# A repeating load for the first norm's weights, scale-and-add steps for three residual rows, and five smaller reorderings in a two-layer hybrid trunk

## The chip, the core and the metric

The kernel runs on one core of one Trainium2 chip. A core has five engines that run their own instruction queues: TensorE (PE, matrix products into PSUM), VectorE (DVE), ScalarE (ACT), GpSimd (POOL) and SyncE (SP, which here issues the transfers). The metric is the device time of one execution in microseconds (us), lower is better; several runs of the kernel are given and the median counts. A profile comes from one execution of its own.

## The reference

Input x is 1024 tokens by 1024 channels in float32. Two layers follow, each `x <- x + RMSNorm_post(mixer(RMSNorm_pre(x)))`:

```python
def rms_norm(x, g):
    y = xf * lax.rsqrt(jnp.mean(xf * xf, axis=-1, keepdims=True) + EPS) * g

def dilated_attention_mixer(h, w_in, w_out, rel_bias):     # layer 0
    proj = h @ w_in                                        # q, k, v for 3 dilations, and a gate z
    ...                                                    # three dilated sliding windows, 16 heads of 64
    o = jnp.sum(wts[..., None] * jnp.stack(outs), axis=0)  # mixed by softmax over the log-sum-exps
    return (o * jax.nn.silu(z)) @ w_out

def s5_mixer(h, w_in, a_re, ..., w_glu, b_glu, w_out):     # layer 1
    u, z = proj[..., :SSM_WIDTH], proj[..., SSM_WIDTH:]
    y = s5_scan(u, ...)                                    # 64 groups of 16 channels, 64 complex states each
    g = jax.nn.gelu(y)
    y = g * jax.nn.sigmoid(g @ w_glu + b_glu)
    return (y * jax.nn.silu(z)) @ w_out
```

## The kernel before

Tokens are worked in eight rows of 128 (row 0 to row 7). Float32 precision is kept by splitting every operand into a high part (an ACT cast to fp32r, L109, L194, L287: `hh`, `whi`) and a low part (a subtraction, L110, L195, L288: `hl`, `wlo`), and by three matmuls per product: high by high, low by high, high by low. The program is one Tile program: a scheduler places the instructions on each engine's queue from data flow, priorities and a simulated timeline, so an edit in one place moves neighbours in others. `issue_after(i)` adds one edge: what is issued inside comes behind instruction `i` on the engine of `i`.

The stages that the change touches, in order of time:

- **The start** (0 to 30 us). Eight transfers of x rows, four quarters of the first value weights `w_v` (`raw_first`), the identity matrix `ident` and the first norm's weights are issued by SP. The norm's weights (1024 numbers) come as two rows of 512 on one partition (`grow`, L1007) and are spread over the 128 partitions by a matmul with a column of ones (`pg`, L1029) and two ACT copies (L182). Six matmuls on zeros (`idle`, L1014) stand on PE before these and six behind. `first_row` (L176) normalises row 0: ACT square with a running sum (L173), the reciprocal root on DVE in nine small steps (`rstd`, L94 to L101), the scaling by root and weights (L189), transposes on PE against `identr` (L152), ACT high part (L194), DVE low part (L195). `first_values` (L273) multiplies each row with the value weights (`psv`, L310), and lets the next rows' norms (`norm_transpose0`) run ahead.
- **Gates and values** (up to 330 us). `gates` projects the branch gate; its weights for four column blocks are loaded and split behind an instruction remembered as `c.behind`. `Quads.values` multiplies the rest of the values with seven products in place of eight, and interleaves jobs of `Prep`, which makes the state-space layer's tables: powers of the transition on DVE and POOL. `Prep.powers(et)` (L1709 ff.) needs block `et` of the input `bc`, loaded at L1650 into one of four work tiles `o[0..3]` or into a spare tile `c.vextra`; o[0] first holds a table that must have been stored to HBM (`tab_dr`, L1639).
- **Attention output** (`out_tiles`, L1232, about 1090 to 1210 us): per row two halves of the output product, then `out_norm` (L1196): ACT squares, `rstd`, DVE `y = ps*r*post` (L1208), POOL `x = x + y` (L1212).
- **The state-space layer** (`layer1`): 32 projection steps, with the stages of eight groups (`ssm_states`, `ssm_outputs`) appended to numbered steps by the list `at`. Group 7 is cut in halves; its second half `ssm_states1` runs at step `LAST_HALF` = 27. A half is: `pv` on PE, three products `T` on DVE, a sum on POOL (L1833), four scans on DVE (L1836), a product on POOL (L1838) and on DVE (L1841), and `X` (L1842), which the output product `py` (L1856) reads. The outputs go through a GELU: ACT (L1857, L1858), POOL (L1859, L1860), ACT tanh (L1861), DVE (L1862).
- **The last output product** (`out_units`, L1363): units of four output rows by seven products; `OutUnit.sums` (L1345) adds the products up in PSUM banks (`ow`, `ox`, `oy`, `oz`) with DVE L1343. All rows but the last use `out_norm` (in the last unit with half of the scaling on ACT L1210 and POOL L1211, `dve=False`), the last one `out_norm_last` (L1215).

Of the kernel before, what the change touches and what calls it, by code (L numbers as in the profile page):

```python
# [24 lines left out]
P = 128  # L25
# [3 lines left out]
H = 512  # L29
# [6 lines left out]

IDLE = 6

# [136 lines left out]

def first_row(c, x, x1, sq, grow, pgs, h, splits):  # L176

    nc = c.nc
    act, dve = Behind(c), Behind(c)
    act(lambda: square(c, 0, x, sq))  # L180
    for b in range(2):
        act(lambda: nc.scalar.copy(grow[:, b * H:b * H + H], pgs[b]))  # L182
    act(splits[0][0])
# [96 lines left out]
def first_values(c, a, rows):  # L280
# [13 lines left out]
    for i in range(8):  # L294
# [17 lines left out]
        with c.tc.issue_after(done[min(i + 2, 7)]):  # L312
            nc.scalar.copy(ev, ps)
        nc.sync.dma_start(c.v_dr[0, 0, i * P:i * P + P], ev)


# [665 lines left out]
def attention(c, a):  # L982
# [4 lines left out]
    with tc.tile_pool(name="vphase", bufs=1, side="right", reuse_waits="tile") as pool:  # L987
# [16 lines left out]

        grow, ones = [c.slot("grow", tag="b")[0:1] for _ in range(2)], c.slot("ones", tag="a")[0:1, 0:P]
        for n, t in enumerate(grow):
            nc.sync.dma_start(t, bass.AP(src.tensor, src.offset + n * H, [[0, 1], [1, H]]))  # L1007

# [7 lines left out]
        wait(IDLE)  # L1016
        nc.vector.memset(ones, 1.0)
        ident = c.slot("ident")[:, 0:P]
        nc.sync.dma_start(ident, a["ident"])
        c.raw_first = [x[:, 2 * n:2 * n + 2] for x in (c.vslot(4, F32), c.vslot(5, F32)) for n in range(2)]  # L1020
        for n in range(4):
            if n == 2:
                load_x(1)
            nc.sync.dma_start(c.raw_first[n], a["w_v"][0, n])
        load_x(2)
        nc.vector.tensor_copy(c.identr, ident)
        pgs = [c.pst.tile([P, H], F32, tag="pst", name="pg") for _ in range(2)]
        for ps, t in zip(pgs, grow):
            last = nc.tensor.matmul(ps, ones, t, start=True, stop=True)  # L1029
        with tc.issue_after(last.ins):  # L1030
            wait(IDLE)

        def rows(i, splits=None):
            if 2 < i + 2 < 8:
                load_x(i + 2)
            if i == 0:
                return first_row(c, xs[0], xs[1], sq, gain, pgs, h[0], splits)
            norm_transpose0(c, i, xs[i], sq, gain, h[i // 4], slice(i % 4 * P, i % 4 * P + P))
# [156 lines left out]

def out_norm(c, pss, post, x, eps=EPS, slot=None, dve=True, bank=None):  # L1196

# [3 lines left out]
    for n in range(2):  # L1201
        nc.scalar.activation(ys[n], pss[n], AF.Square, accum_out=ss[:, n:n + 1])
    r = rstd(c, ss, eps, bank)
    for n in range(2):
        ns = slice(n * H, n * H + H)
        y = ys[n]
        if dve or n == 0:
            nc.vector.scalar_tensor_tensor(y, pss[n], r[:, 0:1], post[:, ns], op0=ALU.mult, op1=ALU.mult)  # L1208
        else:
            nc.scalar.activation(y, pss[n], AF.Copy, scale=r[:, 0:1])  # L1210
            nc.gpsimd.tensor_tensor(y, y, post[:, ns], op=ALU.mult)  # L1211
# [20 lines left out]
def out_tiles(c, g, w, post, res, done, order, late):  # L1232
# [7 lines left out]
    for i in range(8):  # L1240
# [8 lines left out]
        c.nc.sync.dma_start(x, res(i))  # L1249
        out_norm(c, pss[i], post, x)  # L1250
        done(i, x)
# [49 lines left out]
class OutUnit:  # L1301
# [43 lines left out]
    def sums(self, i, slot):  # L1345
# [8 lines left out]
        elif i == 2:  # L1354
            self.add(self.Z, self.p0, self.Z)
        self.done.add(i)
# [4 lines left out]
def out_units(c, y, forms, post, res, done, last, eps, slot):  # L1361
# [13 lines left out]
    for n, (u, i) in enumerate(todo):  # L1375
# [8 lines left out]
        if i in ((3 if u.r == 3 else 4), 2):  # L1384
# [3 lines left out]
            if n + 1 == len(todo):  # L1388
                return out_norm_last(c, pss, post, x, lambda ns: last(x, ns), eps, slot, small)
            out_norm(c, pss, post, x, eps, slot, u.r < 3, small)  # L1390
            done(row, x)
# [201 lines left out]
class Prep:  # L1593
# [4 lines left out]
    def __init__(self, c, a, v):  # L1598
# [44 lines left out]
        self.mask, self.dd = o[2][:, 832:848], o[2][:, 848:864]  # L1643
        nc.vector.tensor_copy(self.mask, c.ident[:, 0:16])
        for n in range(1, 8):
            nc.vector.tensor_tensor(self.mask, self.mask, c.ident[:, 16 * n:16 * n + 16], op=ALU.add)
        self.tmp = o[3][:, 0:576]
        self.raw = {}
        for et, n, t in ((0, 4, o[0]), (4, 1, o[2][:, 576:832]), (5, 1, c.vextra), (6, 2, o[1][:, 0:512])):
            nc.sync.dma_start(t.rearrange("p (e x) -> p e x", e=n), a["bc"][:, et:et + n])  # L1650
# [224 lines left out]
def layer1(c, a, h1, ws):  # L1875
# [20 lines left out]
    for e in range(8):  # L1896
        t = (11 * e + 2) // 4
        for stage, d in ((ssm_loads, (-1, 2)[e] if e < 2 else 3), (ssm_input, 4 + (e == 0)), (ssm_taps, 6),
                         (ssm_states, 6 + (e == 0)), (ssm_outputs, 10)):
            at[t + d + 1].append((stage, e))  # L1900
    at[LAST_HALF + 1].append((ssm_states1, 7))

# [240 lines left out]
```

## Time and profile before

| | before |
|---|---|
| runs | 1593.5, 1597.0, 1595.37 us |
| median | 1595.37 us |
| the profiled execution | 1593.75 us, of which the span 1592.0 us |
| TensorE clock granted in it | 0.998 of full |
| PE busy | 1571.9 us (99%) |
| DVE, ACT, POOL busy | 1092.4, 826.1, 722.7 us |

A row of the timeline reads: start, duration, engine, line, operation, output tile <- input tiles, shape and count, and in brackets the idle time of the engine before it with what ended it. Matmuls overlap in the pipeline, so a matmul's duration is longer than the distance to the next one's start: rows of one kind are paced by their starts. "SPq" rows are the issue of a transfer, not the transfer.

### The profile page before, as it was taken

The numbers are of one execution on the slowest core, as the hardware profiler recorded it, in microseconds if no ns is written. First come the engines' busy times: TensorE is split into PE (matmuls) and PEld (weight loads), VectorE is DVE, ScalarE is ACT, GpSimd is POOL, SyncE is SP. The second block draws the span as 40 slices with busy tenths as digits, with TensorE's granted clock in tenths as the row PEclk, the third lists the DMA queues.
The fourth block names the chain that finished last, engine by engine and source line by source line (L and its number), as shares of the span: only waits on it lengthen the run. The fifth ranks groups of instructions, "written<-read, shape, count | busy, mean of one in ns | idle before, by whom it ended". The sixth has DMA issues, their size and how long they took to land.

```text
span 1592.0 us, 26875 instructions
## 1 busy us (share of the span) xinstructions
PE 1571.9 (99%) x9390; PEld 1327.6 (83%) x9390; DVE 1092.4 (69%) x2588; ACT 826.1 (52%) x2039; POOL 722.7 (45%) x603
## 2 busy tenths in 40 slices
PE   9999999999999999999999999999999999999997
PEld 6889999988888888888888888888888888878876
DVE  8799898945555655655655656659562999858576
ACT  5231223337777677767777677755453233335343
POOL 0000001026568677686777778711220455423466
PEclk9999999999999999999999999999999999999999
DMA  6313444433223333414324333448246888677513
GB/s 260 126 48 113 159 154 134 150 124 91 70 71 106 103 91 105 110 61 115 100 72 122 100 104 106 134 140 246 98 159 187 250 249 248 197 232 243 153 50 136
DMA packets 185808, 219.58 MB, mean 138 GB/s; under 512 B 43059, under 2 KB 139078, under 8 KB 185160
## 3 DMA queue, kind: packets, MB, share of 16 engines
q1 hardware_dynamic: 185672, 217.86, 44.7%
q8 instruction: 74, 1.21, 0.3%
q14 instruction: 62, 0.51, 0.1%
HBM read 158.75 MB, written 59.06 MB: 137 GB/s over the span
## 4 chain that ended last, share of the span: by engine, by line
PE 81%; DVE 8%; DMA 4%; POOL 3%; issue 2%; SPq 1%; ACT 1%; DVEq 0%; POOLq 0%; ACTq 0%
PE x L574 16%; PE psj L135 15%; PE y L574 12%; PE psq L453 10%; PE pso L1181 6%; PE pso L746 5%; PE psl L669 5%; PE pt L697 4%; PE psv L310 2%; PE psb L135 1%; DVE T L1836 1%; PE oz L1338 1%; PE ox L1338 1%; DVE T L1841 1%; PE pst L152 1%
## 5 line engine op out<-in xcount | busy, mean ns | idle before, releaser
L110 POOL TENSOR_TENSOR wqk<-wraw,wqk 128x512 fp32r<-128x512 f32 x161 | 214.0, 1337 | 101.4 <-ACT wqk L109 99.1
L691 ACT ACTIVATE lg<-lg,nm 128x128 f32<-128x128 f32 (+1 forms) x384 | 168.7, 444 | 1.6
L110 DVE TENSOR_TENSOR ph<-pt,ph 128x512 fp32r<-128x512 f32 (+2 forms) x160 | 93.9, 620 | 94.1 <-ACT ph L109 93.8
L574 PE MATMUL x<-v,wqk 128*128 128x512 f32 x576 | 146.4, 402 | 0.7 <-ACT u L587 0.7
L574 PE MATMUL y<-v,wqk 128*128 128x512 f32 x576 | 145.6, 401 | 0.0
L675 DVE CUSTOM_DVE_ANT_0 lg<-psl,T 128x128 f32<-128x128 f32 (+1 forms) x384 | 110.6, 347 | 42.1 <-PE psl L669 41.9
L1688 POOL TENSOR_TENSOR Ks<-Ks,O 128x16 f32<-128x16 f32 x8 | 4.3, 541 | 288.3 <-ACT Ks L1686 266.1
L574 PE MATMUL x<-hh,wqk 128*128 128x512 f32 x384 | 130.7, 401 | 0.0
L574 PEld LDWEIGHTS y<-v,wqk 128*128 128x128 f32 x576 | 105.3, 188 | 24.1
L109 ACT CAST wqk<-wraw 128x512 fp32r<-128x512 f32 x168 | 103.0, 619 | 41.1 <-DVE wraw L554 29.0
L574 PEld LDWEIGHTS x<-v,wqk 128*128 128x128 f32 x576 | 104.2, 188 | 22.8 <-ACT u L587 1.2
L453 PE MATMUL psq<-whi,v 128*128 128x256 f32 x640 | 120.1, 285 | 0.0
L746 PEld LDWEIGHTS pso<-ph,vs 128*128 128x128 f32 x736 | 97.4, 189 | 9.8 <-DVE ph L110 0.5
L135 PE MATMUL psj<-h1h,whi 128*128 128x512 f32 (+1 forms) x272 | 104.2, 388 | 1.1 <-ACT h1h L109 1.1
L746 PE MATMUL pso<-ph,vs 128*128 128x256 f32 (+1 forms) x736 | 103.3, 281 | 0.3 <-DVE ph L110 0.3
L135 PE MATMUL psj<-h1l,whi 128*128 128x512 f32 (+1 forms) x272 | 102.9, 383 | 0.2 <-DVE h1l L110 0.2
L109 ACT CAST ph<-pt 128x512 fp32r<-128x512 f32 (+2 forms) x160 | 78.6, 534 | 46.8 <-PE pt L697 46.4
L453 PEld LDWEIGHTS psq<-whi,v 128*128 128x128 f32 x640 | 99.8, 189 | 1.6 <-issue 1.0
L109 ACT CAST whi<-v 128x1024 fp32r<-128x1024 f32 x35 | 36.7, 1049 | 110.4 <-PE psq L453 87.2
L453 PE MATMUL psq<-wlo,v 128*128 128x256 f32 x320 | 90.6, 284 | 1.3 <-DVE wlo L110 1.3
L574 PEld LDWEIGHTS x<-hh,wqk 128*128 128x128 f32 x384 | 72.2, 188 | 17.6 <-DVE ql L113 0.3
L697 PE MATMUL pt<-identr,lg 128*128 128x128 f32 x560 | 79.4, 274 | 0.0
(351 smaller groups left out, 4384.2 us busy)
## 6 DMA issues: line engine op xcount, KB each, us to landing
wraw<-in_w_in_dram SPq DMA_DIRECT2D x56, 512.0 KB
v<-in_w_v_dram SPq DMA_DIRECT2D x24, 512.0 KB
mw<-wt_dr SPq DMA_DIRECT2D x84, 128.0 KB
vp<-v_dr SPq DMA_DIRECT2D x32, 256.0 KB
wraw<-in_ssm_w_in_dram SPq DMA_DIRECT2D x16, 512.0 KB
v_dr<-v SPq DMA_DIRECT2D x30, 256.0 KB
wfr<-in_ssm_w_out_dram SPq DMA_DIRECT2D x12, 512.0 KB
ca_dr<-ca SPq DMA_DIRECT2D x32, 144.0 KB
```

The source lines that it names most:

```text
L109: c.last_hi = nc.scalar.copy(hi, src).ins
L110: return (engine or nc.vector).tensor_tensor(lo, src, f32(hi), op=ALU.subtract)
L135: nc.tensor.matmul(ps, w[n == 2][:, k * P:k * P + P], h[n == 1][:, k, :], start=first and k == 0 and m == 0, stop=m == len(order) - 1 and ...
L310: nc.tensor.matmul(ps, (lh, ll, lh)[n], (bh, bh, bl)[n], start=m == 0, stop=m == len(order) - 1)
L453: nc.tensor.matmul(o, r[x][:, k, ts], w[y][:, k, :], skip_group_check=True, start=i in (0, 4, 5) and t % 2 == k == n == 0, stop=k == 3 and ...
L574: c.nc.tensor.matmul(ps, w[:, y, b * P:b * P + P], rows[x][:, b, :], start=i in (0, 1, 4) and m == 0, stop=m == len(order) - 1, skip_group ...
L669: nc.tensor.matmul(psl[:, h, o], x[HEADS[h], qs], y[HEADS[h], ks], start=j == js[0] and i == 0, stop=i == 2, skip_group_check=True)
L675: nc.vector.tensor_tensor_reduce(self.lg[u, j][:, h], psl[:, h, o], self.bt[:, h, 256 - w:256], scale=1.0, scalar=-3.0e38, op0=ALU.add, op ...
L691: c.nc.scalar.activation(t, t, AF.Exp, bias=self.nm[:, h, b:b + 1], accum_out=ms[:, col:col + 1])
L697: c.nc.tensor.transpose(pt[:, n * P:(n + 1) * P], self.lg[u, j][:, h, part * P:part * P + P], c.ident)
L746: nc.tensor.matmul(o, l, r, start=n == 0, stop=n == len(jobs) - 1, skip_group_check=True)
L1181: nc.tensor.matmul(ps, x[:, k, ts], y[:, k, cols], start=n == m == 0, stop=n == KT - 1 and m == len(todo) - 1)
```

## The change

Eight edits:

1. `IDLE` 6 becomes 15, and the second batch of idle matmuls goes: one batch of 15 at the start.
2. The first norm's weights are written to all partitions by one transfer whose source repeats (step 0 over 128 partitions, 512 KB written) instead of two 2 KB loads, the matmuls with ones and the two ACT copies.
3. Row 1 of x is loaded ahead of the second quarter of `w_v` instead of ahead of the third.
4. `c.behind` becomes the marker of row 5 at the end of `first_values`, so the gate weights' casts come later on ACT. A mask copy of `Prep` is put behind the same marker.
5. Block 0 of `bc` goes to the spare tile, blocks 1 to 4 to `o[0]`, block 5 to the rest of `o[2]`. Before, blocks 0 to 3 went to `o[0]`, 4 to `o[2]`, 5 to the spare tile.
6. `out_norm` has a `late` form, used for row 7 of the attention output and for row 7 of the last unit: DVE `y = ps*post` before the root is known, then DVE `x = y*r + x` (one scale-and-add per half), and no POOL step.
7. In the last unit the last sum (`oz`) is written to an SBUF tile `zs`, not back to PSUM.
8. At step 27 `ssm_states1` of group 7 comes ahead of the outputs of group 6 instead of behind them.

```diff
-IDLE = 6
+IDLE = 15
...
-def first_row(c, x, x1, sq, grow, pgs, h, splits):
+def first_row(c, x, x1, sq, grow, h, splits):
...
     act(lambda: square(c, 0, x, sq))
-    for b in range(2):
-        act(lambda: nc.scalar.copy(grow[:, b * H:b * H + H], pgs[b]))
     act(splits[0][0])
...
         nc.sync.dma_start(c.v_dr[0, 0, i * P:i * P + P], ev)
+    c.behind = done[5]
...
-        grow, ones = [c.slot("grow", tag="b")[0:1] for _ in range(2)], c.slot("ones", tag="a")[0:1, 0:P]
-        for n, t in enumerate(grow):
-            nc.sync.dma_start(t, bass.AP(src.tensor, src.offset + n * H, [[0, 1], [1, H]]))
+        nc.sync.dma_start(gain, bass.AP(src.tensor, src.offset, [[0, P], [1, D]]))
...
         wait(IDLE)
-        nc.vector.memset(ones, 1.0)
...
         for n in range(4):
-            if n == 2:
+            if n == 1:
                 load_x(1)
             nc.sync.dma_start(c.raw_first[n], a["w_v"][0, n])
         load_x(2)
         nc.vector.tensor_copy(c.identr, ident)
-        pgs = [c.pst.tile([P, H], F32, tag="pst", name="pg") for _ in range(2)]
-        for ps, t in zip(pgs, grow):
-            last = nc.tensor.matmul(ps, ones, t, start=True, stop=True)
-        with tc.issue_after(last.ins):
-            wait(IDLE)
...
-def out_norm(c, pss, post, x, eps=EPS, slot=None, dve=True, bank=None):
+def out_norm(c, pss, post, x, eps=EPS, slot=None, dve=True, bank=None, late=False):
...
+    for n in range(2 if late else 0):
+        nc.vector.tensor_tensor(ys[n], pss[n], post[:, n * H:n * H + H], op=ALU.mult)
     r = rstd(c, ss, eps, bank)
...
+        if late:
+            nc.vector.scalar_tensor_tensor(x[:, ns], y, r[:, 0:1], x[:, ns], op0=ALU.mult, op1=ALU.add)
+            continue
...
-        out_norm(c, pss[i], post, x)
+        out_norm(c, pss[i], post, x, late=i == 7)
...
         elif i == 2:
-            self.add(self.Z, self.p0, self.Z)
+            t = slot("zs") if self.r == 3 else self.Z
+            self.add(t, self.p0, self.Z)
+            self.Z = t
...
-            out_norm(c, pss, post, x, eps, slot, u.r < 3, small)
+            out_norm(c, pss, post, x, eps, slot, u.r < 3, small, late=u.r == 3 and i == 3)
...
-        nc.vector.tensor_copy(self.mask, c.ident[:, 0:16])
+        with c.tc.issue_after(c.behind):
+            nc.vector.tensor_copy(self.mask, c.ident[:, 0:16])
...
-        for et, n, t in ((0, 4, o[0]), (4, 1, o[2][:, 576:832]), (5, 1, c.vextra), (6, 2, o[1][:, 0:512])):
+        for et, n, t in ((0, 1, c.vextra), (1, 4, o[0]), (5, 1, o[2][:, 576:832]), (6, 2, o[1][:, 0:512])):
...
-    at[LAST_HALF + 1].append((ssm_states1, 7))
+    at[LAST_HALF + 1].insert(0, (ssm_states1, 7))
```

The scheduler turns this into other orders on the queues. Three places follow, each as the queue stood before and as it stands now (row numbers left out; after the change the line numbers are one to four lower).

SP's queue at the start of the program, before and then now (`v_126` holds rows 0 and 1 of x, `v_148`, `v_149` and `v_152`, `v_153` the value weights, `v_125` the norm's weights):

```order
L1001 DMA v_126<-in_x_dram 128x1024
L1007 DMA grow<-in_attn_pre_norm_dram 1x512 x2
L1019 DMA ident<-in_ident_dram 128x128
L1024 DMA v_148<-in_w_v_dram 128x1024 x2
L1001 DMA v_126<-in_x_dram 128x1024
L1024 DMA v_149<-in_w_v_dram 128x1024 x2
```

```order
L1000 DMA v_126<-in_x_dram 128x1024
L1004 DMA v_125<-in_attn_pre_norm_dram 128x1024
L1015 DMA ident<-in_ident_dram 128x128
L1020 DMA v_152<-in_w_v_dram 128x1024
L1000 DMA v_126<-in_x_dram 128x1024
L1020 DMA v_152<-in_w_v_dram 128x1024
L1020 DMA v_153<-in_w_v_dram 128x1024 x2
```

A transfer of 512 KB now stands ahead of `ident` and of all weights, and the second x row has gone up by one place.

DVE's queue around the first `powers` job of the table preparation, before and then now (`O_1554` is the tile `o[0]`, `extra` the spare tile, `v_1642` and `v_1633` are value weights whose low part is made):

```order
L430 TENSOR_TENSOR v_687<-v_687,psq 128x512
L1709 TENSOR_TENSOR ca_1872<-O_1554,O_1556 128x576
L1710 TENSOR_TENSOR O_1557<-O_1554,O_1556 128x576
L1712 TENSOR_TENSOR ca_1873<-O_1554,O_1556 128x576
L1709 TENSOR_TENSOR zr<-O_1554,O_1555 128x512
L1712 TENSOR_TENSOR zi<-O_1554,O_1555 128x512
L110 TENSOR_TENSOR wlo<-v_1642,whi 128x1024
```

```order
L1449 TENSOR_TENSOR scr<-O_1548,tabs 128x32
L1708 TENSOR_TENSOR ca_1864<-extra,O_1548 128x576
L1449 TENSOR_TENSOR O_1548<-O_1548,scr 128x32
L1449 TENSOR_TENSOR scr<-O_1548,tabs 128x256
L1709 TENSOR_TENSOR O_1549<-extra,O_1548 128x576
L110 TENSOR_TENSOR wlo<-v_1633,whi 128x1024
L1449 TENSOR_TENSOR O_1547<-O_1547,scr 128x256
```

The first job now reads the spare tile and is spread among the steps that still build the tables (L1449); the second job, on `o[0]`, begins some 30 rows behind the place that the first had.

POOL's queue in the state-space layer at step 27, before and then now (the sum and product of the second half of group 7 are the `T` and `X` rows, the GELU of group 6's outputs the `Y` rows). On PE the four `pv` products of that half moved from behind the sixteen `py` products of group 6 to ahead of them.

```order
L1859 TENSOR_SCALAR Y_15356<-Y_15356 128x512
L1860 TENSOR_TENSOR Y_15356<-Y_15356,Y_15355 128x512
L1859 TENSOR_SCALAR Y_15374<-Y_15374 128x512
L1860 TENSOR_TENSOR Y_15374<-Y_15374,Y_15373 128x512
L1833 TENSOR_TENSOR T_15391<-T_15391,T_15392 128x512
L1838 TENSOR_TENSOR X<-Cg,T_15391 128x4x127
```

```order
L1832 TENSOR_TENSOR T_15347<-T_15347,T_15348 128x512
L1858 TENSOR_SCALAR Y_15368<-Y_15368 128x512
L1858 TENSOR_SCALAR Y_15386<-Y_15386 128x512
L1859 TENSOR_TENSOR Y_15368<-Y_15368,Y_15367 128x512
L1837 TENSOR_TENSOR X<-Cg,T_15347 128x4x127
L1859 TENSOR_TENSOR Y_15386<-Y_15386,Y_15385 128x512
```

The sum of the half now stands ahead of the GELU rows and its product between them.

More of the change, by code (lines that the diff above doesn't have):

```diff
@@ L1036, in rows @@
             if i == 0:
-                return first_row(c, xs[0], xs[1], sq, gain, pgs, h[0], splits)
+                return first_row(c, xs[0], xs[1], sq, gain, h[0], splits)
             norm_transpose0(c, i, xs[i], sq, gain, h[i // 4], slice(i % 4 * P, i % 4 * P + P))
```

## The prediction

> **What bounds the kernel now.** I read the page's busy times and chain first, then PE's timeline for the places where it does not go on at its pace, then the engine that PE waits for at each.
>
> ```profile
> PE 1571.9 (99%) x9390; PEld 1327.6 (83%) x9390; DVE 1092.4 (69%) x2588; ACT 826.1 (52%) x2039; POOL 722.7 (45%) x603
> PE 81%; DVE 8%; DMA 4%; POOL 3%; issue 2%; SPq 1%; ACT 1%; DVEq 0%; POOLq 0%; ACTq 0%
> ```
>
> PE is busy for 1571.9 of 1592.0 us and carries the chain. The change takes no useful matmul away, so it can win only where PE stands still or behind its last matmul: 20.1 us in all. The places that it touches are these, on PE:
>
> ```profile
> 26.84 0.49 PE L310 MATMUL psv<-v,hh 128*128 128x512 f32 x1 [0.24 <-ACT hh L109]
> 28.64 0.66 PE L152 MATMUL pst<-identr,v 128*128 128x128 f32 x4 [1.31 <-DVE hl L110]
> ...
> 189.98 0.38 PE L453 MATMUL psq<-wlo,v 128*128 128x256 f32 x1 [1.26 <-DVE wlo L110]
> ...
> 1204.69 0.50 PE L135 MATMUL psj<-h1h,whi 128*128 128x256 f32 x2 [1.07 <-ACT h1h L109]
> ...
> 1398.04 0.39 PE L1855 MATMUL py<-U,taps 128*128 128x128 f32 x2
> 1400.62 0.49 PE L1856 MATMUL py<-X,CA 128*128 128x128 f32 x2 [2.19 <-DVE X L1842]
> ...
> 1579.73 2.97 PE L1338 MATMUL oz<-f,wo 128*128 128x512 f32 x12
> ```
>
> The brackets count from a matmul's modelled end. From start to start, less a matmul's own pace (1400.62 - 1398.04 less some 0.22), the loss is 0.1 to 0.2 us larger: 2.36 us at 1398, 1.4 at 188, 1.6 at 27. PE's last matmul ends at 1582.70, the span 9.3 us later: the tail.
>
> **The start (edits 1 to 4).** The rows of three engines and of the view by windows:
>
> ```profile
> 1.45 2.92 PE L1014 MATMUL idle<-zeros 128*128 128x512 f32 x6 [1.45 <-DVE zeros L1010]
> 10.74 1.91 PE L152 MATMUL pst<-identr,v 128*128 128x128 f32 x8
> 25.57 1.03 PE L152 MATMUL pst<-identr,v 128*128 128x128 f32 x8
> ...
> 7.96 1.54 DVE L189 SCALAR_TENSOR_TENSOR v<-v,rs_y,v 128x512 f32<-128x512 f32 x2
> 25.50 2.35 DVE L110 TENSOR_TENSOR wlo<-wraw,whi 128x1024 fp32r<-128x1024 f32 x2
> ...
> 10.27 1.06 ACT L173 ACTIVATE v<-v 128x1024 f32<-128x1024 f32 x1 [0.61 <-DMA v<-in_x_dram]
> 11.23 0.19 ACT L173 ACTIVATION_READ_ACCUMULATOR v<-v 128x1 f32 x1
> 11.83 0.59 ACT L194 CAST hh<-pst 128x512 fp32r<-128x512 f32 x1 [0.41 <-PE pst L152]
> ...
> 8.00:10.20 2.20, 2.20 (x6) 1.80 (x6) 1.98 (x3) 1.53 (x2) 0.00 (x0) 1.00 1.02 419
> 1504.50:1507.00 2.50, 2.50 (x13) 2.01 (x12) 2.50 (x5) 2.50 (x6) 0.00 (x0) 1.00 0.42 139
> ```
>
> The two last rows are of the view by windows; the last figures are the share of the transfer engines and GB/s. From 8 us on the transfers run at 419 GB/s with no gap, so 512 KB cost 524288/419000 = 1.25 us. The repeating load puts 512 KB more ahead of `ident` and every weight. No load before 20 us repeats, but the last norm's weights (issued at 1501.82) come in the same way: while they arrive, the rate is 139 GB/s, at which 512 KB would take 3.8 us. So 1.25 to 3.8 us; I take 2.2, since part of that window is the transfer's first latency, which in a queue lies under its neighbours. Row 1 of x waited until 10.2 behind two weight quarters; it now has one quarter less ahead and the norm's weights more: 10.2 - 1.25 + 2.2 = 11.2 (10.2 to 12.8). ACT then does its square and sum (1.06 and 0.19 with overlap, 1.15) and, behind it in its queue, row 0's high part, which began at 11.83: now at about 12.3. Before, the transposes ahead of it were held by the idle matmuls until 10.74; now by the row's scaling on DVE, which needs weights (about 7) and root, and ends near 9 to 10. So row 0 is 0.5 us later (0 to +2.0) by the loads. Against it: the two ACT copies (0.59 each) go, and the gate weights' low parts (2.35 us at 25.50) no longer stand ahead of row 2's on DVE. But in the new DVE order the scalings of rows 2, 3 and 4 (two halves each, as the pair of 1.54 at L189) stand there, so of the 1.6 us at 27 I count only 0.2 as gained. Sum of the start: +0.3 (-0.8 to +1.8).
>
> [...] Row 0's eight transposes took 1.91 us at 10.74, the same eight at 25.57 took 1.03: the array was slow until then, though the window from 8.00 shows PE busy in all of its 2.20 us. [...]
>
> **The tables (edit 5).**
>
> ```profile
> 175.79 0.33 SPq L1639 DMA_DIRECT2D tab_dr<-O  x1
> 181.08 0.33 SPq L1650 DMA_DIRECT2D O<-in_bc_dram  x1
> ...
> 185.49 0.76 DVE L1709 TENSOR_TENSOR ca<-O,O 128x576 f32<-128x576 f32 x1 [1.98 <-DMA O<-in_bc_dram]
> 188.71 1.22 DVE L110 TENSOR_TENSOR wlo<-v,whi 128x1024 fp32r<-128x1024 f32 x1
> ```
>
> DVE waits 1.98 us for the block that is loaded into `o[0]` after that tile's store, does five products (3.2 us to 188.71), and the low part of a weight queued behind them is 1.26 us late for PE. Now block 0 lies in the spare tile, loaded early, and its job is spread over the table steps before. What is late next could be the second job, which reads `o[0]`. It ran at 206.79 (row below) and stands now with the table steps lengthened by the first job's some 8 us; I put its need at 199 to 207 and the landing at 185.5 + 8 = 193.5, since the load still follows the store of the finished table. That leaves 5 us (estimate).
>
> ```profile
> 206.79 0.76 DVE L1709 TENSOR_TENSOR ca<-O,O 128x576 f32<-128x576 f32 x1 [0.47 <-PE pk L1683]
> ```
>
> So the stall goes: -1.4, at best -1.6 with a shorter DVE queue; 0 if the wait only moves.
>
> **The attention output's row 7 (edit 6).**
>
> ```profile
> 1193.39 2.53 POOL L1212 TENSOR_TENSOR xr<-xr,y 128x512 f32<-128x512 f32 x2 [11.31 <-DMA xr<-in_x_dram]
> ...
> 1200.89 1.34 ACT L228 ACTIVATE xn<-xr,rs_y 128x512 f32<-128x512 f32 x2 [1.56 <-DVE rs_y L101]
> 1202.59 1.04 PE L152 MATMUL pst<-identr,xn 128*128 128x128 f32 x8
> 1203.29 1.29 DVE L232 TENSOR_TENSOR xn<-pst,gcol 128x512 f32<-128x512 f32 x2 [2.50 <-PE pst L152]
> ```
>
> POOL's two sums (2.53) become two DVE steps of about 0.75 each (1.41 for a pair at L1228, below), from the same landing of `xr`: the row is ready 1.0 us earlier. But PE's stall at 1204.69 does not hang on it: the normalised row is there at 1202.2, PE comes to its transposes at 1202.59 by its own queue, and the wait is for the transposes' way through DVE and ACT. 0 (-0.5 if the scheduler's order lets the transposes up, +0.3 if the DVE steps delay other low parts).
>
> **The second half of group 7 (edit 8).**
>
> ```profile
> 1387.49 0.69 DVE L1832 TENSOR_TENSOR T<-Sg,pv 64x512 f32<-64x512 f32 x1
> ...
> 1389.20 1.75 POOL L1860 TENSOR_TENSOR Y<-Y,Y 128x512 f32<-128x512 f32 x1
> 1390.91 1.30 POOL L1833 TENSOR_TENSOR T<-T,T 128x512 f32<-128x512 f32 x1
> ...
> 1394.59 0.69 DVE L1862 SCALAR_TENSOR_TENSOR Y<-Y,Y 128x512 f32<-128x512 f32 x1 [4.79 <-ACT Y L1861]
> 1395.20 1.36 DVE L1836 TENSOR_TENSOR_SCAN T<-rho,T 128x128 f32<-128x128 f32 x4
> ```
>
> The half's inputs are ready at 1388.2, its sum waits on POOL behind the GELU until 1390.91, ends at 1392.2, and its scans stand on DVE behind L1862, which waits 4.79 us for ACT. From scan to `X` (1399.59 + 0.98) it is 5.4 us, and PE needs `X` at 1398.2. Now the sum comes at 1388.2 to 1389.5 and the scans at once, to 1391.0; POOL does two GELU scalings (0.62 each) and one product (1.75) and then L1838 (1.70), ending at 1394.2; `X` is done by 1395.2, 3 us before PE asks. The whole stall goes: -2.35. The GELU's second product is now behind L1838, about 1.5 us later than before; it feeds a store whose reload is for a later stage. If the scans' wait merely shortened by the sum's 2.7 us while they stayed behind L1862, nothing would be won (0); so the range is -2.5 to 0, and I take the full value, since POOL's new order stands fixed.
>
> **The tail (edits 6 and 7).**
>
> ```profile
> 1582.30 0.75 DVE L1208 SCALAR_TENSOR_TENSOR post<-ox,rs_y,post 128x512 f32<-128x512 f32 x1
> 1583.03 0.69 DVE L1343 TENSOR_TENSOR oz<-p,oz 128x512 f32<-128x512 f32 x1
> 1584.60 0.69 DVE L1223 TENSOR_TENSOR post<-oz,post 128x512 f32<-128x512 f32 x1 [0.89 <-ACT sq L1222]
> 1585.20 0.15 DVE L96 SCALAR_TENSOR_TENSOR rs<-ss,rs 128x1 f32<-128x1 f32 x1
> 1587.22 1.41 DVE L1228 SCALAR_TENSOR_TENSOR xr<-post,rs_y,xr 128x512 f32<-128x512 f32 x2
> 1586.86 0.34 SPq L2051 DMA_DIRECT2D out_dram<-xr  x1
> 1588.00 0.99 SPq L2052 DMA_DIRECT2D out_dram<-xr  x2
> ```
>
> PE ends at 1582.70. DVE comes to the `oz` sum 0.33 us later, behind L1208; its product L1223 then stands idle for 0.89 us, because ACT squares the same PSUM bank. Now L1208 is not there (-0.3) and the sum goes to SBUF, so the product follows it at once (-0.9). But row 7's two scale-and-adds (1.41) now stand between that product and L96: 1585.20 - 0.33 - 0.89 + 1.41 = 1585.4, and L94 moves behind them too (0.2): 1585.6, so the last pair L1228 begins 0.4 later. Against it row 7's store (L2051, 512 KB) no longer waits for POOL's 2.49 us and is issued 1.3 earlier; it took the transfer engines that the last stores (L2052) wanted, worth 0.2. Sum +0.2 (0 to +0.6).
>
> **The sum.** +0.3 - 1.4 + 0 - 2.35 + 0.2 = -3.25 us; The glu and gate stages, whose orders move too, count 0 (-0.6 to +0.6): PE's timeline shows no wait there that the edits touch. Against the profiled execution's 1593.75 us that is 1590.5. That run is 1.6 below the median 1595.37; from the median it is **1592.1 us**.
>
> **The rivals.** Differences under 0.2% (3.2 us) can hardly be told from none, and the forecast stands on that line.
>
> A: as summed, 1592.1, its own range 1590.6 to 1593.7. Chance 0.50.
>
> B: the start wins as well. The gate weights leave row 2's path wholly and both stalls at 27 us go (-1.6 more, less my 0.2), and row 7 gets its transposes up at 1204 (-0.5): 1590.2 or less, down to 1588. For: the 2.35 us of weight splits that stood at 25.50 on DVE are gone from there. Against: the L212 rows in their place. Chance 0.14. [...]
>
> C: one of the two large terms only moves. Either the scans meet another wait (ACT's queue, 4.79 us before L1862, speaks for it; their new place for its absence), then +2.35; or the second `powers` job waits for `o[0]`, +1.4. 1593.5 to 1595.4. For: both sums rest on orders, not on a trace. Chance 0.27. That the mask's new edge does nothing (the marker is on ACT, the copy on DVE) and that row 7's step at 1203 does nothing is in all cases.
>
> D: slower. The repeating load is the mechanism: 128 reads of one 4 KB source, with `ident`, row 1 and all weights behind it. Each us that it takes beyond 2.2 moves `ident` and row 1, and from there row 0, one for one. The sum of -3.25 is eaten up at 2.2 + 3.25 = 5.45 us (96 GB/s), and the kernel is slower by 0.2% at 8.65 us (61 GB/s). For: the slowest window of its kind, 139 GB/s. Against: 3.8 us by that rate. 1595.4 to 1599, chance 0.09.
>
> **How the numbers follow.** Faster by over 0.2% (below 1592.2): half of A, a little over since its open ends lean down (0.28), B (0.14), and 0.05 for a start that gains with C: 0.47. Slower by over 0.2% (above 1598.6): 0.05 of D. Within: the rest, 0.48. The range of 8 in 10 reaches from B's middle, 1588.6, to the end of C with a little of D, 1595.8.
>
> **What would show it.** On PE: no bracket at the first `psq` matmuls behind the first table job, and the `py` pairs of the second half of group 7 going at 0.22 us without a pause; if instead a bracket with DVE `wlo` or DVE `X` stands there, C is right. On POOL the sum of that half should start within 0.2 us of the third `T` product, before the GELU rows. At the start: row 0's first high part on ACT at 12.3 (11.8 to 13.8) and the third row's stall near 27 to 29 us still of 1 us or more; without it, B. The wait of DVE's `identr` cast for `ident`, which was at 5.4, shows the length of the repeating load: past 10 speaks for D. At the end L1228's pair should start some 4.9 us behind PE's last matmul (4.5 before). The forecast is wrong if PE's idle time falls by less than 2 us or by more than 6.

## The result, and the profile after

| | before | changed |
|---|---|---|
| median of 19 runs | 1593.84 us | 1588.9 us |
| lowest to highest | 1591.55 to 1597.0 | 1587.02 to 1595.73 |
| span of the profiled execution | 1592.0 | 1587.4 |

The ratio is 0.9972, 95% interval 0.9964 to 0.9980: 0.28% shorter, 4.5 us. Forecast were -3.25 us, in a range that holds the result. The forecast counted from the median of the three runs known then, 1595.37; over nineteen runs the kernel before has 1593.84. The two large terms came near what was written, the start did not; the account below goes by the two profiled executions, whose difference is 4.6 us.

The changed kernel's page, its busy times and its chain:

```profile
PE 1570.2 (99%) x9389; PEld 1328.5 (84%) x9389; DVE 1103.9 (70%) x2592; ACT 822.6 (52%) x2036; POOL 710.7 (45%) x598
PE 92%; DMA 3%; DVE 2%; issue 1%; POOL 1%; ACT 0%; SPq 0%; DVEq 0%; POOLq 0%; ACTq 0%
```

TensorE's share of the chain went from 81 to 92%. Its idle time fell by 2.9 us (from 20.1 to 17.2) and its busy time by 1.7. To see where, TensorE's own marks were set side by side (the start or end of the same matmul in both timelines, us):

| mark on TensorE | before | changed | shift | moved since the mark above |
|---|---|---|---|---|
| first product of row 0 starts | 12.47 | 11.32 | -1.15 | -1.15 |
| first value stage ends | 66.44 | 67.24 | +0.80 | +1.95 |
| attention units start | 330.77 | 328.98 | -1.80 | -2.60 |
| attention output ends | 1184.12 | 1181.63 | -2.49 | -0.69 |
| state-space outputs end | 1402.45 | 1397.55 | -4.90 | -2.41 |
| last matmul ends | 1582.70 | 1577.79 | -4.91 | 0.0 |
| span ends | 1592.0 | 1587.4 | -4.6 | +0.3 |

The changed kernel's timeline at the start, TensorE first, then the engines that feed it:

```profile
1.45 6.44 PE L1011 MATMUL idle<-zeros 128*128 128x512 f32 x15 [1.45 <-DVE zeros L1007]
9.19 1.32 PE L152 MATMUL pst<-identr,v 128*128 128x128 f32 x8 [1.30 <-DVE v L187]
11.32 0.80 PE L308 MATMUL psv<-v,hh 128*128 128x512 f32 x1 [0.81 <-ACT hh L192]
...
16.47 0.63 PE L308 MATMUL psv<-v,hl 128*128 128x512 f32 x1
16.90 0.63 PE L308 MATMUL psv<-v,hh 128*128 128x512 f32 x1
17.33 0.52 PE L308 MATMUL psv<-v,hl 128*128 128x512 f32 x1
17.69 0.40 PE L308 MATMUL psv<-v,hh 128*128 128x512 f32 x1
17.92 0.40 PE L308 MATMUL psv<-v,hl 128*128 128x512 f32 x1
...
28.76 0.50 PE L308 MATMUL psv<-v,hh 128*128 128x512 f32 x1 [0.24 <-ACT hh L109]
29.49 0.66 PE L152 MATMUL pst<-identr,v 128*128 128x128 f32 x4 [0.22 <-DVE hl L110]
...
6.87 0.23 DVE L1022 CAST identr<-ident 128x128 fp32r<-128x128 f32 x1 [0.41 <-DMA ident<-in_ident_dram]
9.64 1.06 ACT L173 ACTIVATE v<-v 128x1024 f32<-128x1024 f32 x1 [0.28 <-DMA v<-in_x_dram]
10.70 0.57 ACT L192 CAST hh<-pst 128x512 fp32r<-128x512 f32 x1
```

Row 0's high part comes at 10.70 instead of 11.83, but its products then go at 0.43 us from start to start until 17.33 (half pace), and only from 17.69 on at 0.23 (full pace). The view by windows of the changed kernel, in stretches of 3.41 us, shows why (columns: length and busy time of PE; PEld, DVE, ACT, POOL; then the granted TensorE clock, the share of the transfer engines and GB/s):

```profile
7.36:10.77 3.41, 1.84 (x11) 0.93 (x9) 3.41 (x14) 2.18 (x4) 0.00 (x0) 1.00 1.02 419
10.77:14.18 3.41, 2.86 (x6) 2.04 (x7) 3.34 (x11) 3.41 (x6) 0.00 (x0) 0.50 1.03 414
14.18:17.60 3.42, 3.42 (x9) 2.65 (x9) 3.42 (x10) 2.71 (x5) 0.00 (x0) 0.50 1.02 408
```

The array had come to full pace at 7.36, as the idle matmuls ended (the transposes at 9.19 go at 0.11 us each). The stretch that followed was busy for 1.84 of 3.41 us, and at its end the clock was halved, for two stretches. Fourteen products at 0.43 instead of 0.23 us are 2.75 us (an estimate from these rows): more than the 1.15 us that the earlier start had won.

At 188 us there is no wait any more: VectorE makes the low part at 183.88, and TensorE takes it at 188.53 without a pause.

```profile
183.88 1.23 DVE L110 TENSOR_TENSOR wlo<-v,whi 128x1024 fp32r<-128x1024 f32 x1
188.53 0.28 PE L452 MATMUL psq<-wlo,v 128*128 128x256 f32 x1
```

At the second half of group 7:

```profile
1385.69 1.29 POOL L1832 TENSOR_TENSOR T<-T,T 128x512 f32<-128x512 f32 x1 [5.76 <-DVE T L1831]
1390.30 1.80 POOL L1837 TENSOR_TENSOR X<-Cg,T 128x508 f32<-128x508 f32 x1 [0.36 <-DVE T L1835]
...
1387.02 3.20 DVE L1835 TENSOR_TENSOR_SCAN T<-rho,T 128x128 f32<-128x128 f32 x4 [1.41 <-POOL T L1832]
1394.27 0.67 DVE L1841 TENSOR_TENSOR X<-X,T 128x508 f32<-128x508 f32 x1
...
1395.60 0.39 PE L1854 MATMUL py<-U,taps 128*128 128x128 f32 x2
1395.83 0.39 PE L1855 MATMUL py<-X,CA 128*128 128x128 f32 x2
```

The sum is done right behind the third `T` product, and no `py` product waits: the pair at 1395.60, the ninth of its block, is the one that stood 2.36 us before. In the tail:

```profile
1579.23 1.41 DVE L1201 SCALAR_TENSOR_TENSOR xr<-post,rs_y,xr 128x512 f32<-128x512 f32 x2
1580.82 0.16 DVE L96 SCALAR_TENSOR_TENSOR rs<-ss,rs 128x1 f32<-128x1 f32 x1
1582.79 1.41 DVE L1224 SCALAR_TENSOR_TENSOR xr<-post,rs_y,xr 128x512 f32<-128x512 f32 x2
1580.67 0.34 SPq L2050 DMA_DIRECT2D out_dram<-xr  x1
1583.56 0.99 SPq L2051 DMA_DIRECT2D out_dram<-xr  x2
```

The last pair starts 5.0 us behind TensorE's last matmul (before: 4.5), with row 7's two steps ahead of its chain.

### The profile page after: what moved, and what is told of

Read it like the earlier page. It is cut to its first block, busy times and chain, and to the rows that moved or that the text cites. A ratio compares the mean times of both kernels' runs of the same rounds, so it can differ in the third digit from the quotient of the medians.

```text
span 1587.4 us, 26865 instructions
## 1 busy us (share of the span) xinstructions
PE 1570.2 (99%) x9389; PEld 1328.5 (84%) x9389; DVE 1103.9 (70%) x2592; ACT 822.6 (52%) x2036; POOL 710.7 (45%) x598
## 4 chain that ended last, share of the span: by engine, by line
PE 92%; DMA 3%; DVE 2%; issue 1%; POOL 1%; ACT 0%; SPq 0%; DVEq 0%; POOLq 0%; ACTq 0%
PE psj L135 21%; PE x L573 16%; PE psq L452 13%; PE y L573 12%; PE pso L1172 6%; PE pso L745 5%; PE psl L668 5%; PE pt L696 4%; PE psv L308 2%; PE psb L135 1%; PE oz L1334 1%; PE py L1855 1%; PE py L1854 1%; PE pv L1828 1%; PE ox L1334 1%
## 5 line engine op out<-in xcount | busy, mean ns | idle before, releaser
L109 ACT CAST wqk<-wraw 128x512 fp32r<-128x512 f32 x168 | 103.0, 619 | 42.9 <-DVE wraw L553 30.8
```

What stands on the lines that cost most here:

```text
L109: c.last_hi = nc.scalar.copy(hi, src).ins
```

## The experiments

Three questions were open: what the start lost and to what; which edit took the waits at 27, 114 and 188 us away; and what each of the late edits is worth. Twelve kernels were timed, one of them the changed kernel again. Those of the last section apart, each is the changed kernel with one edit or group of edits undone, or one thing altered. The marks (us; "value stage" is the end of the first value stage, "middle" the time from the first `psq` product of the later values, near 111, to the first attention unit, "wait at 1452" TensorE's lost time in the glu stage, which follows the state-space outputs, "tail" the time from the last matmul to the end of the span):

| kernel | value stage | wait of row 2 | middle | wait at 1452 | tail | span |
|---|---|---|---|---|---|---|
| before | 66.44 | 1.57 | 219.7 | 0 | 9.3 | 1592.0 |
| changed | 67.24 | 0.50 | 217.1 | 0 | 9.6 | 1587.4 |
| changed, second profile | 65.80 | 0.49 | 217.1 | 0 | 9.6 | 1585.4 |
| kept busy at the start | 65.66 | 0.60 | 217.1 | 2.74 | 9.6 | 1590.3 |
| edit 8 undone | 66.79 | 0.50 | 217.1 | 3.79 | 9.6 | 1594.7 |
| edit 5 undone | 65.79 | 0.50 | 217.1 | 0.50 | 9.6 | 1586.2 |
| edits 1 to 3 undone | 65.91 | 1.10 | 218.2 | 0 | 9.6 | 1587.2 |
| edit 4 undone | 69.25 | 2.55 | 217.5 | 0 | 9.6 | 1589.0 |
| edits 4 and 5 undone | 69.35 | 2.69 | 219.1 | 0 | 9.6 | 1591.8 |
| row 7 of the attention output undone | 65.97 | 0.54 | 217.1 | 3.51 | 9.6 | 1592.7 |
| last unit's edits undone | 66.28 | 0.54 | 217.1 | 0.49 | 9.3 | 1586.1 |

The spans alone can't be compared: two waits that no edit aims at, at the start and at 1452, move them by more than an edit is worth. The marks can.

**The clock at the start.** More idle matmuls, so that TensorE is hardly idle before row 0:

```diff
-IDLE = 15
+IDLE = 22
...
         ps = transpose_half(c, x[:, b * H:b * H + H])
+        if b == 1:
+            with c.tc.issue_after(c.last_pst.ins):
+                c.wait(3)
```

> The changed kernel with 22 idle matmuls at the start instead of 15 and 3 more behind row 0's transposes, so that TensorE is hardly idle before row 0's products. Theory 1 (the clock): the changed kernel lost about 2.7 us at the start because its array, at full pace for the transposes at 9.19, was set back to half pace at 10.77 and made 14 products of row 0 at 0.427 instead of 0.231 us; kept busy, the products go at 0.23 us from the first, row 0 ends near 17.5 instead of 20.0, and the end of the first value stage (67.24 us in the changed kernel) comes 1.5 to 2.5 us earlier; the whole is 1.5 to 2.5 us shorter than the changed kernel, so 6 to 7 us (0.4%) shorter than the kernel before. Theory 2 (data): row 1 waits for its norm on VectorE and for its load anyway; the stage ends at most 0.5 us earlier and the whole stays at 4 to 5 us below the kernel before.

The value stage ended at 65.66, 1.6 us earlier, within theory 1's 1.5 to 2.5. It is not the whole 2.75, since in this kernel's order VectorE makes row 0's first low part at 12.34, not at 11.30, and TensorE waits for it:

```profile
13.08 0.50 PE L311 MATMUL psv<-v,hl 128*128 128x512 f32 x1 [1.11 <-DVE hl L196]
```

But the median was 1591.73 (10 runs; the kernel before beside it 1592.33; ratio 0.9997, 0.9986 to 1.0008): the total of theory 1 was wrong. This kernel lost 2.7 us at 1452 and ran at half pace for 3.4 us behind it, in the profiled execution:

```profile
1451.46:1454.88 3.42, 0.84 (x5) 0.36 (x3) 2.07 (x4) 1.82 (x3) 0.00 (x0) 1.00 0.88 338
1454.88:1458.30 3.42, 3.42 (x8) 2.66 (x9) 3.08 (x5) 2.31 (x4) 0.33 (x1) 0.50 1.02 352
```

**The start's edits together.** Edits 1 to 3 undone (two batches of six idle matmuls with the products of ones between them, the weights copied by ACT, the second x row behind two weight quarters), edit 4 kept.

> The changed kernel with edits 1 to 3 undone (two batches of 6 idle matmuls, weights of the norm by matmul, second x row behind two weight quarters), gate weights still late. Theory 1 (the clock): as in the kernel before, the array is at full pace from about 13.4 on; the first value stage then ends 0.5 to 1.5 us earlier than in the changed kernel (67.24), so the three edits lost time. Theory 2 (the load order): the three edits brought row 0's first high part forward by 1.1 us and are worth that; without them the stage ends 1 us later.

The value stage ended at 65.91: 1.3 earlier than in the changed kernel's first profile and 0.1 later than in its second. Over the seven profiles with the changed kernel's own start (edit 4 kept) it ended at 65.8 to 67.4: at 67.24 in the changed kernel's first, where the half pace lasted two stretches (10.77 to 17.60), at 65.80 in its second, where it lasted one (11.07 to 14.49). So edits 1 to 3 cost between nothing and 1.5 us there: theory 1 by the first profile, neither theory by the second, and the 1.15 us of earlier products is real too. In exchange the middle was 1.0 longer without them: the wait of 0.65 at 114 (0.55 before; the bracket names DVE's gate product) is theirs to have removed. From the attention output's end to that of the state-space outputs it was 0.75 longer as well, with a stall of 1.3 at the second half of group 7. The median, 1588.62 (ratio 0.9975, 0.9965 to 0.9985), is about that of the whole change, so these three edits are worth nothing that the runs could show.

**Which edit took the wait at 188.** Edit 5 alone undone:

```diff
-        for et, n, t in ((0, 1, c.vextra), (1, 4, o[0]), (5, 1, o[2][:, 576:832]), (6, 2, o[1][:, 0:512])):
+        for et, n, t in ((0, 4, o[0]), (4, 1, o[2][:, 576:832]), (5, 1, c.vextra), (6, 2, o[1][:, 0:512])):
```

> The changed kernel with edit 5 alone undone (blocks 0 to 3 of bc in the first work tile again). Theory 1: VectorE waits for the block's load again and TensorE loses 1.3 to 1.6 us near 188; the small losses at 114 (0.55) and 291 (0.44), which the changed kernel lacks, stay away. Rival: those two hang on the blocks' places as well, then the loss between 100 and 330 us is 2.2 to 2.6 us.

Neither theory held: nothing came back, the middle stayed 217.1. With the old blocks, DVE waits 0.19 us for the load and the weight's low part stands ahead of the wait:

```profile
182.42 1.23 DVE L110 TENSOR_TENSOR wlo<-v,whi 128x1024 fp32r<-128x1024 f32 x1
183.84 0.76 DVE L1708 TENSOR_TENSOR ca<-O,O 128x576 f32<-128x576 f32 x1 [0.19 <-DMA O<-in_bc_dram]
```

Edit 4 alone undone (the line `c.behind = done[5]` taken out):

> The changed kernel with edit 4 alone undone (gate weights right behind row 0 again). Theory 1, after the block order turned out to be worth nothing: the gate weights' early casts and low parts are what disturbed VectorE's order both at 27 us (1.6 us lost) and, by their places in the queue, at 114 and 188; undone, TensorE loses 1 us or more at 27 and at least 0.5 us more between 100 and 330 us. Rival: edit 4 only matters at 27 us; then 0.5 to 1.6 us there and nothing near 188.

The rival's mechanism held, with more than its 1.6 us: 2.05 us more at row 2, and nothing at 188 (the middle 0.3 longer).

```profile
28.63 0.51 PE L308 MATMUL psv<-v,hh 128*128 128x512 f32 x1 [0.24 <-ACT hh L109]
31.41 0.66 PE L152 MATMUL pst<-identr,v 128*128 128x128 f32 x4 [2.28 <-DVE hl L110]
```

Both undone:

> The changed kernel with edits 4 and 5 both undone. Undoing one of them alone brought no stall back near 188 us. Theory 1: either is enough to take that stall away; with both undone TensorE loses 1.2 to 1.6 us there again, beside 2.5 at 29. Rival: the stall hung on the simulated times of the old start, which decide where the scheduler puts the first table job's products against the weights' low parts; then nothing is lost at 188 here either.

```profile
187.55 0.76 DVE L1707 TENSOR_TENSOR ca<-O,O 128x576 f32<-128x576 f32 x1 [1.66 <-DMA O<-in_bc_dram]
190.77 1.22 DVE L110 TENSOR_TENSOR wlo<-v,whi 128x1024 fp32r<-128x1024 f32 x1
192.04 0.39 PE L451 MATMUL psq<-wlo,v 128*128 128x256 f32 x1 [0.94 <-DVE wlo L110]
```

Theory 1 held: the load's wait, the five products and the late low part are all back. TensorE lost 1.1 us at 190.8, a little under the 1.2 to 1.6 expected, and 0.6 at 293. Either edit is enough to take this wait away: edit 5 by the early block, edit 4 by another DVE order in which the low part comes first.

**Edit 8 undone** (`append` again).

> The changed kernel with edit 8 alone undone (the second half of group 7 behind the outputs of group 6 again). Theory 1: the stall of 2.36 us at the second half of group 7 comes back in full and nothing else moves: the span is 2.3 to 2.5 us above the changed kernel's. Rival: the stall's size depends on what came before, and ACT's casts come at another time now; then the stall is under 1 us.

The result lies between the two: a stall of 1.60 us came back, for `X` as before, and from the attention output's end to that of the state-space outputs the kernel needed 1.7 us more than the changed one.

```profile
1394.95 0.39 PE L1854 MATMUL py<-U,taps 128*128 128x128 f32 x2
1396.78 0.49 PE L1855 MATMUL py<-X,CA 128*128 128x128 f32 x2 [1.44 <-DVE X L1841]
```

The whole change shortened that stretch by 2.4 us. The 0.75 us that came back without edits 1 to 3 are about the difference; the two were not undone together. Afterwards this kernel lost 3.79 at 1454, and the total says nothing.

**Row 7 of the attention output** as before (`late` off there).

> The changed kernel with edit 6 undone in the attention output only (row 7 by GpSimd's sums again). Theory 1: TensorE's stalls near 1201 (1.23 and 0.39) come from the way of the transposed row through VectorE and ScalarE, and are the same without the edit: within 0.1 us. Rival: the edit did shorten a wait that would have grown by now; then the two are 0.5 us or more longer.

The changed kernel's row, then this kernel's:

```profile
1202.24 0.50 PE L135 MATMUL psj<-h1h,whi 128*128 128x256 f32 x2 [1.07 <-ACT h1h L109]
```

```profile
1201.27 0.50 PE L135 MATMUL psj<-h1h,whi 128*128 128x256 f32 x2 [1.07 <-ACT h1h L109]
```

Theory 1 held to the hundredth: the edit is worth nothing there, as forecast.

**The last unit's edits undone** (`oz` back in PSUM, row 7 by ACT and POOL).

> The changed kernel with the two edits of the last unit undone (sum of oz back in PSUM, row ahead of the last by ScalarE and GpSimd). Theory 1: the tail from TensorE's last matmul to the end of the span, 9.6 us in the changed kernel, is 9.2 to 9.3 as in the kernel before, so the two edits cost 0.3 to 0.4. Rival: in the changed kernel the tail is longer for another reason, and stays at 9.6.

The tail is 9.3 again. In every kernel above that has the two edits it is 9.6: together they cost 0.33 us; which of them does was not tried. (Edit 6 gives the new steps to two rows; the third row that works so, the very last, did so before.)

**The wait at 1452.** The product `zg` (L1951) on VectorE:

```diff
-        nc.gpsimd.tensor_tensor(z, z, y, op=ALU.mult)
+        nc.vector.tensor_tensor(z, z, y, op=ALU.mult)
```

> The changed kernel with the product of the gate and the state-space output in the glu stage (L1951) on VectorE instead of GpSimd. Theory 1 (shared time of GpSimd and VectorE): in two of four traces this product took 4.3 and 5.4 us on GpSimd instead of 1.3 while VectorE ran without a gap; it held back VectorE, then SP's loads behind it, and TensorE stood 2.7 and 3.8 us near 1452 and was set back to half pace for 3.4 and 6.8 us. On VectorE no such stall comes in any run: the slow runs of the changed kernel (1592.7, 1595.6, 1595.7 of 19) disappear, all runs lie within 2.5 us of each other and the median is 1587.5 to 1588.5. Rival: the stall is the transfer's own lateness; then runs above 1592 remain.

Five runs gave 1588.35 to 1588.96, median 1588.71 (ratio 0.9965, 0.9952 to 0.9978), with no wait at 1452 in the profile and the runs within 0.6 us of each other; the median is a little above the forecast. So few runs can't show that those above 1592 are gone: the changed kernel had three of them in nineteen runs, and none in six others. What happens at the wait, in the kernel with edit 8 undone, shows in these rows: GpSimd's product, the load that DVE and ACT wait for, and TensorE:

```profile
1443.82 5.41 POOL L1951 TENSOR_TENSOR zg<-zg,yg 128x512 f32<-128x512 f32 x1 [3.45 <-DMA zg<-z_dr]
...
1449.27 0.69 DVE L1954 SCALAR_TENSOR_TENSOR yb<-tg,zg 128x512 f32<-128x512 f32 x1 [1.19 <-POOL zg L1951]
1456.48 0.69 DVE L1267 TENSOR_TENSOR wfr<-wfr 128x512 f32<-128x512 f32 x1 [5.32 <-DMA wfr<-in_ssm_w_out_dram]
1456.48 0.62 ACT L109 CAST f1h<-wfr 128x512 fp32r<-128x512 f32 x1 [8.42 <-DMA wfr<-in_ssm_w_out_dram]
...
1458.46 3.78 PE L135 MATMUL psj<-g0b,whi 128*128 128x512 f32 x8 [3.63 <-ACT tg L1953]
```

The product takes 5.41 us where the changed kernel's profile has 1.38 (at 1442.65). DVE's next step waits for it, SP's loads behind it go out 3 to 4 us later than in the changed kernel, ACT's cast of the weights stands ahead of the tanh that empties TensorE's bank, and TensorE waits. Of eleven profiles with `zg` on GpSimd, four have this product (the sixth of sixteen) at 4.3 to 5.4 us, the others at 1.3 to 1.5. (Of the four traces that the expectation speaks of these are three, not two.) In the kernel with edit 8 undone and in the one kept busy at the start it ended 1.15 us behind the last of a row of VectorE steps without gaps (1449.23 against 1448.08, 1446.61 against 1445.46). Three of the four are those with a wait of 2.7 us or more here, each with TensorE at half pace behind it: the granted clock was 0.50 in these two kernels, and in the one without row 7's edit five matmuls took 2.50 us where eight had taken 2.04. The fourth, with edits 1 to 3 undone, has none:

```profile
1441.77 5.16 POOL L1961 TENSOR_TENSOR zg<-zg,yg 128x512 f32<-128x512 f32 x1 [3.70 <-DMA zg<-z_dr]
...
1451.02 0.62 ACT L109 CAST f1h<-wfr 128x512 fp32r<-128x512 f32 x1 [4.88 <-DMA wfr<-in_ssm_w_out_dram]
```

There SP's loads of the weights went out at 1447.42, and ACT had the weights at 1451.02; in the kernel with edit 8 undone it was 1450.16 and 1456.48. So no long wait came without a slow product, but a slow product is not enough, and what else decides is not shown. The seven profiles with a fast product have 0 to 0.5 us of wait. In the three with `zg` on VectorE (this one and the two versions below) there is none.

**A better version?** The start kept busy, `zg` on VectorE, and the row ahead of the last scaled on ACT and added on POOL:

> The changed kernel with three edits: TensorE kept busy at the start (22 idle matmuls and 3 behind the transposes, as before), the glu product on VectorE, and the row ahead of the last scaled on ScalarE and added on GpSimd instead of two scale-and-add steps on VectorE. Theory 1: -1.5 at the start, no stall at 1452, and -0.5 to -1.0 in the tail: 1586.0 to 1587.0, 0.4% below the kernel before and 0.1% below the changed kernel's usual run. Rival: the tail is set by the last stores together, then the tail gains nothing and it is 1586.7 to 1587.5.

The median was 1588.33 us (five runs, 1587.81 to 1589.1; ratio 0.9964, 0.9952 to 0.9977). The value stage ended at 65.58, and no wait came at 1452, but the tail became 9.9, worse than the rival had it, for row 7's store now went out at 1581.15, together with the last two at 1581.70. With the tail of the kernel before instead, beside the changed kernel on the same chip:

> TensorE kept busy at the start, the glu product on VectorE, and the tail as in the kernel before (the two edits of the last unit undone). Theory 1: the tail is 9.3 us after TensorE's last matmul instead of 9.6 or the 9.9 of the version with ScalarE and GpSimd, the start is 1.5 us shorter than the changed kernel's: the profiled span is 1585.5 to 1585.9, and the median is 1.3 to 2 us below the changed kernel's of the same call. Rival: the gain at the start is taken back at a later wait; then the two medians are within 0.7 us.

> The changed kernel as it is, to be timed beside the version above. Both theories: 1588 to 1589.5 in its usual runs; by the theory of GpSimd and VectorE, two or three runs in nineteen above 1592 with a stall near 1450, by the rival none that the profile could tell.

The medians were 1587.97 (ratio 0.9960, 0.9947 to 0.9974) against the changed kernel's 1588.44 (ratio 0.9964, 0.9951 to 0.9977). The profiled spans are 1584.7 and 1585.4, the tail is 9.3 as expected, and in the version's profile TensorE kept its full pace through row 0's transposes and products (granted clock 1.00 in the stretches below and up to 30 us, 0.998 over the span):

```profile
7.83:11.24 3.41, 2.28 (x13) 1.30 (x11) 3.36 (x12) 2.70 (x5) 0.00 (x0) 1.00 1.02 416
11.24:14.66 3.42, 2.39 (x9) 1.61 (x9) 3.26 (x10) 3.31 (x4) 0.00 (x0) 1.00 1.03 416
```

But the medians differ by 0.5 us, within the rival's 0.7: in the profile the changed kernel's half pace lasted one stretch only, which costs little (value stage 65.80 against 65.29), it had no wait at 1452, and none of its six runs was above 1589.1. Whether this version is faster than the changed kernel is not settled by these runs.

## Why the prediction was right, step by step

The total came inside the range (-3.25 forecast, -4.5 measured), but near its edge and in part by luck. From the median of nineteen runs the same sum would have given 1590.6; measured were 1588.9, 0.3 above the low end of the range, 1588.6, and below case A's 1590.6 to 1593.7. The forecast started from three runs with a median 1.5 us higher, and this is why 1592.1 lies so far off. In the two profiles the sum missed -1.2 in the middle and -0.7 in the attention units, against +0.5 at the start and +0.1 in the tail.

- **The start, +0.3 forecast, +0.8 measured in the profile and -0.6 in the changed kernel's second one**, by other causes than written. The repeating load was priced at 2.2 us between 1.25 and 3.8: `ident` came 1.5 us later than before (6.87 against 5.37), so the repeating 512 KB cost about as much as plain ones (1.25 us at the 419 GB/s of the kernel before). With the second x row one place up, row 0's high part came at 10.70, not at 12.3: -1.1 instead of +0.5. The sum has no term for the clock: behind a stretch with gaps of 1.3 and 0.8 us it was halved (0.50), and the price was 2.75 us of slow products. And the gate weights were credited with 0.2: row 2's wait is 2.55 without edit 4 and 0.50 with it in the new start, 1.57 and 1.10 in the old one, so edit 4 is worth 2.05 or 0.5, and the L212 rows that I put in their place on DVE did not hold up row 2. In the profile -1.15 (row 0), -1.07 (row 2) and +2.75 come to +0.5 of the +0.8; the rest was not traced. That these errors nearly cancelled is luck: where the half pace lasted one stretch only, as in the second profile, they did not. Case B's sign came (no wait of 1 us at 27 to 29), and the median lies among B's times, but not by B's sum: the clock took the gain at the start, and row 7 gained nothing.
- **The tables, -1.4 forecast, -1.4 measured at 188**, and another 1.0 at 114 and 291 that the sum left out. The step that named edit 5 as the cause was half right: edit 4 does the same. The second `powers` job on `o[0]` began at 203.60, inside the 199 to 207 written, and did not wait for its load.
- **Row 7 of the attention output: 0**, as forecast and for the reason given.
- **Edit 8, -2.35 forecast, -2.4 measured for the stretch.** But undoing edit 8 alone gave 1.7 of it back, not all: the step that put the whole stall down to edit 8 was too simple. The cover was thinner than written, too: the four scans took 3.20 us beside POOL's GELU steps, not 1.36, and `X` was ready at 1394.9, 0.7 us before TensorE asks (the pair at 1395.60), not 3. With the old start, edit 8 in place, TensorE's block began 1.5 us earlier, `X` came 0.6 later, and TensorE lost 1.3 us there.
- **The tail, +0.2 forecast, +0.33 measured**: L1228's pair starts 5.0 us behind the last matmul (4.9 written). From there to the end it took 4.61 us instead of 4.74, so the earlier store of row 7, credited with 0.2 without a row, brought 0.13 at most.
- **Not in the sum**: 0.7 us in the attention units (the wait at 859 was 1.1 before, 0.46 after, and 0 to 0.6 in the other kernels, which all have the same order there). That the edits did it is not shown.

## What to carry to other kernels

A wait that either of two edits takes away looks like the work of whichever was read first; only undoing them singly and together tells it. Before TensorE has its real work, count its gaps too, those between idle matmuls and first products: here a stretch of 3.41 us that was busy for 1.84 was followed by half clock, and the slow products cost 2.75 us where the earlier start had won 1.15. And a step on GpSimd beside a VectorE queue without gaps had no reliable time here (1.3 to 5.4 us). Where something waits for it, try it elsewhere: here that left no long wait in three profiles, though no gain in the median that the runs could show.

## What the hardware showed that was not expected

- **The granted clock was halved behind four stretches in which TensorE was busy for 0.25 to 0.54 of the time.** In the changed kernel's first profile it was 0.50 from 10.77 to 17.60, twice 3.41 us. Seven stretches of about that length at clock 1.00, by how busy TensorE was in them, with the clock of what followed:

| kernel | stretch | TensorE busy | share | clock behind it |
|---|---|---|---|---|
| kept busy at the start | 1451.46 to 1454.88 | 0.84 of 3.42 | 0.25 | 0.50 |
| edits 4 and 5 undone | 27.4 to 30.8 | 0.97 of 3.40 | 0.29 | 0.50 |
| changed, second profile | 7.66 to 11.07 | 1.68 of 3.41 | 0.49 | 0.50 |
| edit 4 undone | 27.11 to 30.53 | 1.78 of 3.42 | 0.52 | full pace (products 0.23 us apart from 32.14) |
| changed | 7.36 to 10.77 | 1.84 of 3.41 | 0.54 | 0.50 |
| before | 187.48 to 190.89 | 2.15 of 3.41 | 0.63 | 1.00 |
| the last version above | 7.83 to 11.24 | 2.28 of 3.41 | 0.67 | 1.00 |

The shares overlap (0.54 was followed by half clock, 0.52 was not), by records whose matmul ends are modelled; a limit is not shown. The stretch of the kernel without edit 4:

```profile
27.11:30.53 3.42, 1.78 (x11) 1.12 (x9) 3.38 (x6) 2.54 (x5) 0.92 (x1) 1.00 0.43 134
```

- **A GpSimd product took up to four times as long beside VectorE's steps.** The same 128x512 product took 1.3 to 1.5 us in seven profiles, and 4.3, 5.2, 5.3 and 5.4 us in four; in two of these four, with edit 8 undone and kept busy at the start, it stood beside VectorE steps of 0.68 us in a row and ended 1.15 us after the row did. When it went through in 1.38 us, the VectorE step beside it took 1.78 instead of 0.68 (changed kernel, 1442.79). So either was longer beside the other, VectorE by 1.1 us and GpSimd by 4.1. The runs show these times alone; what causes them is not shown.
